# Holding back the taps of a long convolution while stick-breaking weights are worked out, and issuing them more densely around that

## The chip, the cores and the metric

The kernel runs on one core of a Trainium2 chip. The metric is the device time of one execution in microseconds (us). Three executions before the change took 883.54, 887.52 and 886.16 us; their median is 886.16 us. One further execution was profiled.

## What is computed

One layer of an encoder over 512 positions of width 1024. Four branches mix the positions in parallel; what they give is gated, projected, merged and normalised. Two branches matter here: the Conformer convolution, a causal depthwise convolution of 31 taps over 512 channels, and stick-breaking attention with 8 heads of width 64.

```python
g_lin, g_gate = jnp.split(glu, 2, axis=-1)
hB = g_lin * jax.nn.sigmoid(g_gate)
hB = causal_dwconv(hB, conv_dw) + conv_dw_bias      # 31 taps
...
z = jnp.einsum('bhqd,bhsd->bhqs', qi, kh) * scale   # stick-breaking
log_beta = jax.nn.log_sigmoid(z)
log_rest = jnp.where(mask, jax.nn.log_sigmoid(-z), 0.0)
between = lax.cumsum(log_rest, axis=3, reverse=True) - log_rest
att = jnp.where(mask, jnp.exp(log_beta + between), 0.0)
```

## The kernel before, in words

Channels lie on the 128 partitions and the 512 positions along the free axis. Every large projection is done with split operands: a matrix is rounded to a high half (`hi`, on ACT, L108) and the remainder is its low half (`lo`, L109, on DVE, or on POOL for every second piece while `shared[0]` is set), and three products are summed (`mm3`, L121 to L123). A step of a projection is three matmuls of 512 columns. The weights stream in from HBM by SP's queue.

The order of the work is written as generators. `todo` is a list of projections; each `next` of one of them issues a step of three matmuls. `fill(n)` issues n such steps. `chain(gen)` runs a serial computation and calls `fill` with the number that the computation yields, so that TensorE has projection work while it waits for the other engines. Attention is such a computation: `pair` (L730) works on two heads at a time, four pairs in a branch, and yields after each of its three banks of scores (`f1`, 4 steps each and 6 more at the end) and after each of three groups of transposes (`f2_`, 2 steps each and 2 more). Between two pairs `attention` (L799) calls `fill(FB)`, 14 steps.

The convolution's taps ride on `fill`. A tap is one DVE instruction over up to 512 elements (L308 for the first, L310 for the others, `oB` += `hB` shifted times a weight); there are 31 for each of four channel groups, each adding to what the one ahead of it wrote. They wait in the list `taps`, and `fill` pays a fixed share of a tap for every step, in `due`:

```python
if taps:
    due[0] += RATE
    while due[0] >= 1 and taps:
        due[0] -= 1
        taps.pop(0)()
```

With RATE 0.5 one tap goes out for two steps. The taps stand in program order on DVE by `keep_in_program_order`; a scheduler settles the rest of DVE's order.

For a stick-breaking pair the weights of the two heads are worked out in a chain over ACT and DVE. For each bank and head ACT forms two sigmoids from the scores (`rs`, L750, and `a`, L751), DVE runs a reversed cumulative product over `rs` (the scan, L770) and multiplies it into `a` (L771). `rs` has a single buffer, so the next `rs` on ACT waits for the last multiply on DVE. The banks are the 512 long rows, then the 128 and 384 long ones, then the 256 long ones. When the weights stand, TensorE transposes them (L781), ACT copies the transposes, and L796 multiplies them by the values; DVE's L797 takes the result. L665 on DVE multiplies a gated projection into `merged`. L709 and L713 are the low halves of the next pair's queries and keys.

Of the kernel before, what the change touches and what calls it, by code (L numbers as in the profile page):

```python
# [23 lines left out]
F1, F2, FB, FL = (4, 6), (2, 2), 14, (24, 24)  # L24

FE = (10, 2, 8, 34, 2)

RATE = 0.5
O_QA, O_KA, O_VA, O_ZA, O_AA, O_BA = 0, 512, 1024, 1536, 2048, 2052
O_LIN, O_GLU, O_ZB = 2056, 2568, 3080  # L30
O_QC, O_KC, O_VC, O_ZC = 3592, 4104, 4616, 5128
# [45 lines left out]
def trunk(ctx, tc, xT, pT, wi, ws, wb, wo, wg, wp, cst, colp, ln, out):  # L77
# [14 lines left out]
    def nm(p):  # L92
        cnt[0] += 1
        return f"{p}_{cnt[0]}"

    def bank(shape=(128, 512)):
        return psW.tile(list(shape), F32, tag="w", name=nm("w"))
# [45 lines left out]

    taps, due = [], [0.0]

    def fill(n):
        while n > 0 and todo:
            try:
                next(todo[0])
                n -= 1  # L150
                if taps:
                    due[0] += RATE
                    while due[0] >= 1 and taps:
                        due[0] -= 1
                        taps.pop(0)()
            except StopIteration:
                todo.pop(0)

    def finish(gen):

        while gen in todo:
            fill(1)

    def chain(gen):
        for n in gen:
            fill(n)

    def b4(col):
        return col.unsqueeze(2).to_broadcast([128, 4, 128])
# [219 lines left out]
    nc.vector.tensor_tensor(Fst[32:40, :], fc, Fst[0:8, :].bitcast(F32), ALU.subtract)  # L389

    fill(FE[0])
    cum = bank()
    g16f = g16.rearrange("p a b -> p (a b)")
# [103 lines left out]
    def double(cs_):  # L497
# [4 lines left out]
        for i in range(4, 7):  # L502
# [19 lines left out]
            yield 1  # L522

    chain(double((0, 1)))
    chain(double((2, 3)))
    finish(vq[3])

# [172 lines left out]
    def heads(name, pr):  # L700

        pcs = unit(name, pr)
        fox = name == "qkD"
        qs = -0.125 if fox else 0.125
        t = [at.tile([128, T], F32R, tag=n, name=nm(n), bufs=2) for n in ("qh", "ql", "kh", "kl")]

        def qthen(ps):
            nc.scalar.activation(t[0], ps, AF.Copy, scale=qs)
            nc.vector.scalar_tensor_tensor(t[1], ps, qs, t[0].bitcast(F32), ALU.mult, ALU.subtract)  # L709

        def kthen(ps):
            nc.scalar.activation(t[2], ps, AF.Copy)
            nc.vector.tensor_tensor(t[3], ps, t[2].bitcast(F32), ALU.subtract)  # L713

        yield from proj(pcs, 0, qthen)
        yield from proj(pcs, 1, kthen)
        qk[name, pr] = t
        if fox:

            both = base.tile([128, 4, T], F32, tag="oB" if pr % 2 else "hB", name=nm("F"))  # L720
            plain, diag = both[:, 0:2, :], both[:, 2:4, :]
            for hh in range(2):
                ps = acc()
                h = 2 * pr + hh
                mm(ps, lhsT=selr[:, h:h + 1].to_broadcast([128, 128]), rhs=Fst, start=True, stop=True)
                nc.scalar.activation(plain[:, hh, :], ps, AF.Copy)
                nc.gpsimd.tensor_tensor(b3(diag[:, hh, :]), b3(plain[:, hh, :]), h4(far), ALU.add)
            bias[pr] = plain, diag

    def pair(name, pr, v, dst, f1, f2_):  # L730

        fox = name == "qkD"
        qh, ql, kh, kl = qk[name, pr]
        att, aT = {}, {}
        for segs in BANKS:
            pss = [bank(), bank()]
            for i, o in segs:
                n = 128 * (i + 1)
                tq = slice(128 * i, 128 * i + 128)
                for lq, lk in ((qh, kh), (qh, kl), (ql, kh)):  # L740
                    for hh in range(2):
                        ro = slice(64 * hh, 64 * hh + 64)
                        mm(pss[hh][:, o:o + n], lhsT=lq[ro, tq], rhs=lk[ro, 0:n], start=lq is qh and lk is kh, stop=lq is ql)  # L743
            w = max(o + 128 * (i + 1) for i, o in segs)
            for hh in range(2):
                ps = pss[hh]
                a = at.tile([128, T], F32, tag="a", name=nm("a"), bufs=6)
                if not fox:
                    rs = at.tile([128, T], F32, tag="rs", name=nm("rs"), bufs=1)
                    nc.scalar.activation(rs[:, 0:w], ps[:, 0:w], AF.Sigmoid, scale=-1.0)  # L750
                    nc.scalar.activation(a[:, 0:w], ps[:, 0:w], AF.Sigmoid)  # L751
                for i, o in segs:
                    n = 128 * (i + 1)
                    d = o + n - 128
                    if fox:

                        st = at.tile([128, 4], F32, tag="st", name=nm("st"), bufs=6)
                        fp, fd = bias[pr]
                        if i:
                            nc.vector.tensor_tensor_reduce(a[:, o:d], ps[:, o:d], fp[:, hh, 0:n - 128], 1.0, BIG, ALU.add, ALU.min, st[:, 0:1])  # L760
                        nc.vector.tensor_tensor_reduce(a[:, d:o + n], ps[:, d:o + n], fd[:, hh, n - 128:n], 1.0, st[:, 0:1] if i else BIG,
                                                       ALU.add, ALU.min, st[:, 1:2])
                        nc.scalar.activation(a[:, o:o + n], a[:, o:o + n], AF.Exp, bias=st[:, 1:2], scale=-1.0, accum_out=st[:, 2:3])
                        nc.vector.reciprocal(st[:, 3:4], st[:, 2:3])
                        nc.vector.tensor_scalar(a[:, o:o + n], a[:, o:o + n], st[:, 3:4], None, ALU.mult)
                    else:


                        rv = rs[:, o + 1:o + n][:, ::-1]
                        nc.vector.tensor_tensor_scan(rv, rv, last[:, 512 - n:511][:, ::-1], 0.0, ALU.mult, ALU.add)  # L770
                        nc.vector.tensor_tensor(a[:, o:o + n - 1], a[:, o:o + n - 1], rs[:, o + 1:o + n], ALU.mult)  # L771
                        nc.gpsimd.memset(a[:, o + n - 1:o + n], 0.0)
                    att[hh, i] = a[:, o:o + n]
            yield f1[0]
        yield f1[1]
        for n_, segs in enumerate(TBANKS):
            for hh in range(2):
                ps = bank()
                for j, o in segs:
                    for i in range(j, 4):  # L780
                        nc.tensor.transpose(ps[:, o + 128 * (i - j):o + 128 * (i - j) + 128], att[hh, i][:, 128 * j:128 * j + 128], ident)  # L781
                w = max(o + 128 * (4 - j) for j, o in segs)
                t = at.tile([128, T], F32, tag="aT", name=nm("aT"), bufs=6)
                if hh and fox:
                    nc.vector.tensor_copy(t[:, 0:w], ps[:, 0:w])
                else:
                    nc.scalar.activation(t[:, 0:w], ps[:, 0:w], AF.Copy)
                for j, o in segs:
                    aT[hh, j] = t[:, o:o + 128 * (4 - j)]
            yield f2_[0]  # L790
        yield f2_[1]
        po = bank()
        for j in range(4):
            for hh in range(2):
                c0 = 128 * pr + 64 * hh
                mm(po[64 * hh:64 * hh + 64, 128 * j:T], lhsT=v[:, j, c0:c0 + 64], rhs=aT[hh, j], start=j == 0, stop=j == 3)  # L796
        nc.vector.tensor_tensor(dst[:, pr, :], po, dst[:, pr, :], ALU.mult)  # L797

    def attention(name, v, dst, others, first=lambda: None):  # L799
        hs = [heads(name, pr) for pr in range(4)]  # L800
        todo.append(hs[0])
        for pr in range(4):
            finish(hs[pr])
            if pr == 0:
                first()
            if pr < 3:
                todo.append(hs[pr + 1])
            todo.append(others(pr))
            chain(pair(name, pr, v, dst, F1, F2))
            if pr < 3:  # L810
                fill(FB)

    def once(f):
        got = []
# [7 lines left out]
    fill(9999)  # L822

    attention("qkC", v, zC, lambda pr: gates(0, pr, ysA, False, 0))
    while taps:
        taps.pop(0)()
# [43 lines left out]
    todo.append(zbgate())  # L870
    ysB = once(lambda: ysplit(oB, True))
    attention("qkD", v, zD, lambda pr: gates(1, pr, ysB, True, 1), ysB)
    fill(9999)
    s2.close()
# [164 lines left out]
```

## Time and profile before

| | us |
|---|---|
| median of three runs | 886.16 |
| the profiled execution | 883.57 |
| its span, first to last instruction | 881.5 |
| TensorE busy | 850.9 (97%) |
| VectorE (DVE) busy | 552.8 (63%) |
| ScalarE (ACT) busy | 332.7 (38%) |
| GpSimd (POOL) busy | 143.9 (16%) |

A busy share is an average over stages. The four stick-breaking pairs lie between 278 and 416 us of the span. Times in the rows are microseconds from the span's start, and a group's mean is in nanoseconds. L12 is line 12 of the kernel.

### The profile page before, as it was taken

Reading aid. Unit: us, or ns where it says so; the run is one execution under the profiler, and the core shown is the slowest. Engines: PE = TensorE matmul, PEld = TensorE weight load, DVE = VectorE, ACT = ScalarE, POOL = GpSimd, SP = SyncE. Lnnn points to the kernel's source line nnn. Section 1 sums busy time; section 2 is a strip of 40 time slices with the busy share of each in tenths; the row PEclk is TensorE's granted clock in tenths of the full one; section 3 lists DMA queues with packets and bytes.
Section 4 is the critical chain, followed back from the end, with each engine's and each line's share of the span. In section 5 each row is a group of like instructions: output and inputs, shape, how many; then the busy total and the mean of one; then the engine's idle time right before and its main releaser. Section 6 shows DMA issues by size and latency. Waiting matters only on the chain.

```text
span 881.5 us, 11299 instructions
## 1 busy us (share of the span) xinstructions
PE 850.9 (97%) x4364; PEld 685.6 (78%) x4364; DVE 552.8 (63%) x931; ACT 332.7 (38%) x588; POOL 143.9 (16%) x137
## 2 busy tenths in 40 slices
PE   7989999999999999999999999999999999999996
PEld 5767789988897676677898777777788888888885
DVE  4999845569895888886433546374633434454367
ACT  5754322432233444434243434352423323333220
POOL 0453200221122021110122211111111111200021
PEclk9999999999999999999999999999999999999998
DMA  7434411002232121132122312232322222354202
GB/s 253 144 94 128 115 59 49 25 28 93 96 111 96 49 71 52 69 120 72 48 96 96 120 48 72 72 120 72 120 72 92 99 96 74 117 159 152 72 14 83
DMA packets 33653, 79.75 MB, mean 90 GB/s; under 512 B 7104, under 2 KB 13888, under 8 KB 33472
## 3 DMA queue, kind: packets, MB, share of 16 engines
q1 hardware_dynamic: 31152, 73.73, 24.8%
q10 hardware_dynamic: 2448, 5.31, 1.9%
q8 instruction: 34, 0.56, 0.3%
q14 instruction: 19, 0.16, 0.1%
HBM read 74.70 MB, written 4.33 MB: 90 GB/s over the span
## 4 chain that ended last, share of the span: by engine, by line
PE 82%; DVE 10%; issue 2%; ACT 2%; DMA 2%; POOL 2%; SPq 0%; DVEq 0%; ACTq 0%; POOLq 0%
PE p L121 19%; PE p L122 18%; PE p L123 18%; PE w L121 5%; PE w L123 5%; PE w L122 5%; PE w L796 2%; PE w L781 2%; PE w L743 2%; PE w L182 2%; DVE rs L770 1%; PE w L511 1%; PE w L519 1%; DVE lo L109 1%; DVE cacc L272 1%
## 5 line engine op out<-in xcount | busy, mean ns | idle before, releaser
L121 PE MATMUL p<-xhi,hi 128*128 128x512 f32 x656 | 265.8, 405 | 0.0
L122 PE MATMUL p<-xlo,hi 128*128 128x512 f32 x656 | 260.0, 396 | 0.0
L123 PE MATMUL p<-xhi,lo 128*128 128x512 f32 x656 | 259.9, 396 | 0.0
L109 DVE TENSOR_TENSOR lo<-raw,hi 128x1024 fp32r<-128x1024 f32 x114 | 152.2, 1336 | 99.6 <-ACT hi L108 90.3
L108 ACT ACTIVATE hi<-raw 128x1024 fp32r<-128x1024 f32 x124 | 131.0, 1059 | 217.2 <-PE p L122 160.1
L121 PEld LDWEIGHTS p<-xhi,hi 128*128 128x128 f32 x656 | 123.4, 188 | 32.4 <-issue 4.3
L123 PEld LDWEIGHTS p<-xhi,lo 128*128 128x128 f32 x656 | 123.2, 188 | 29.3 <-issue 0.4
L122 PEld LDWEIGHTS p<-xlo,hi 128*128 128x128 f32 x656 | 123.5, 188 | 26.5 <-issue 0.6
L310 DVE SCALAR_TENSOR_TENSOR oB<-hB,cp,oB 128x511 f32<-128x511 f32 (+14 forms) x120 | 97.8, 815 | 2.3
L667 POOL TENSOR_TENSOR merged<-merged,sg 128x512 f32<-128x512 f32 x24 | 34.2, 1427 | 185.1 <-DVE sg L665 113.9
L121 PE MATMUL w<-yh,hi 128*128 128x512 f32 x128 | 51.8, 405 | 0.0
L122 PE MATMUL w<-yl,hi 128*128 128x512 f32 x128 | 50.5, 395 | 0.0
L123 PE MATMUL w<-yh,lo 128*128 128x512 f32 x128 | 50.5, 394 | 0.0
L109 POOL TENSOR_TENSOR lo<-raw,hi 128x1024 fp32r<-128x1024 f32 x10 | 25.5, 2553 | 122.3 <-ACT hi L108 74.8
L665 DVE TENSOR_TENSOR sg<-w,sg 128x512 f32<-128x512 f32 x16 | 11.1, 691 | 41.7 <-PE w L123 41.7
L121 PE MATMUL p<-hi,xhi 128*128 128x256 f32 x128 | 35.8, 280 | 0.0
L770 DVE TENSOR_TENSOR_SCAN rs<-rs,masks 128x511 f32<-128x511 f32 (+3 forms) x32 | 28.6, 913 | 11.5 <-ACT rs L750 11.5
L122 PE MATMUL p<-lo,xhi 128*128 128x256 f32 x128 | 35.7, 279 | 0.0
L123 PE MATMUL p<-hi,xlo 128*128 128x256 f32 x128 | 35.7, 279 | 0.0
L121 PEld LDWEIGHTS w<-yh,hi 128*128 128x128 f32 x128 | 24.0, 188 | 6.3 <-issue 1.0
L123 PEld LDWEIGHTS w<-yh,lo 128*128 128x128 f32 x128 | 24.1, 188 | 5.7
L781 PE MATMUL w<-ident,a 128*128 128x128 f32 x160 | 22.6, 274 | 5.9 <-DVE a L771 5.9
(298 smaller groups left out, 1270.9 us busy)
## 6 DMA issues: line engine op xcount, KB each, us to landing
raw<-wi SPq DMA_DIRECT2D x90, 512.0 KB, 3.2
raw<-wb SPq DMA_DIRECT2D x16, 512.0 KB, 3.2
raw<-wo SPq DMA_DIRECT2D x8, 512.0 KB, 3.1
raw<-wg SPq DMA_DIRECT2D x8, 512.0 KB, 3.3
t<-xT ACTq DMA_DIRECT2D x8, 256.0 KB, 3.3
xr<-xT SPq DMA_DIRECT2D x3, 512.0 KB, 5.5
dX<-Q SPq DMA_DIRECT2D x4, 256.0 KB, 2.6
dL<-L SPq DMA_DIRECT2D x4, 256.0 KB, 2.2
```

The lines of the kernel that those rows point to most:

```text
L108: nc.scalar.activation(hi, raw, AF.Copy)
L109: eng.tensor_tensor(lo, raw, hi.bitcast(F32), ALU.subtract)
L121: mm(ps, lhsT=wh, rhs=ah, start=first, stop=False)
L122: mm(ps, lhsT=wh, rhs=al, start=False, stop=False)
L123: mm(ps, lhsT=wl, rhs=ah, start=False, stop=last)
L182: nc.tensor.transpose(ps[:, 128 * h:128 * h + 128], src(h), idn)
L310: i = nc.vector.scalar_tensor_tensor(a[:, s:], h[:, :T - s], cw31[:, c, 30 - s:31 - s], a[:, s:], ALU.mult, ALU.add)
L667: nc.gpsimd.tensor_tensor(merged[:, d, :], merged[:, d, :], sg, ALU.add)
L743: mm(pss[hh][:, o:o + n], lhsT=lq[ro, tq], rhs=lk[ro, 0:n], start=lq is qh and lk is kh, stop=lq is ql)
L770: nc.vector.tensor_tensor_scan(rv, rv, last[:, 512 - n:511][:, ::-1], 0.0, ALU.mult, ALU.add)
L781: nc.tensor.transpose(ps[:, o + 128 * (i - j):o + 128 * (i - j) + 128], att[hh, i][:, 128 * j:128 * j + 128], ident)
L796: mm(po[64 * hh:64 * hh + 64, 128 * j:T], lhsT=v[:, j, c0:c0 + 64], rhs=aT[hh, j], start=j == 0, stop=j == 3)
```

## The change

`fill` takes the rate as a second argument. While a stick-breaking or forgetting pair works out its weights (the `f1` yields), the rate is HELD, 0: no tap goes out. In the transposes (`f2_`) and in the stretch between pairs (`FB`) it is FREE, 0.9, in place of 0.5. Everywhere else it stays RATE, 0.5. The forgetting branch runs when no taps are left, so that only the stick-breaking branch sees it. The number of taps, of matmuls and of all other instructions is the same.

```diff
--- before.py
+++ after.py
@@ -25,7 +25,7 @@
 
 FE = (10, 2, 8, 34, 2)
 
-RATE = 0.5
+RATE, HELD, FREE = 0.5, 0.0, 0.9
 O_QA, O_KA, O_VA, O_ZA, O_AA, O_BA = 0, 512, 1024, 1536, 2048, 2052
 O_LIN, O_GLU, O_ZB = 2056, 2568, 3080
 O_QC, O_KC, O_VC, O_ZC = 3592, 4104, 4616, 5128
@@ -143,13 +143,13 @@
 
     taps, due = [], [0.0]
 
-    def fill(n):
+    def fill(n, rate=RATE):
         while n > 0 and todo:
             try:
                 next(todo[0])
                 n -= 1
                 if taps:
-                    due[0] += RATE
+                    due[0] += rate
                     while due[0] >= 1 and taps:
                         due[0] -= 1
                         taps.pop(0)()
@@ -163,7 +163,7 @@
 
     def chain(gen):
         for n in gen:
-            fill(n)
+            fill(*n) if isinstance(n, tuple) else fill(n)
 
     def b4(col):
         return col.unsqueeze(2).to_broadcast([128, 4, 128])
@@ -771,8 +771,8 @@
                         nc.vector.tensor_tensor(a[:, o:o + n - 1], a[:, o:o + n - 1], rs[:, o + 1:o + n], ALU.mult)
                         nc.gpsimd.memset(a[:, o + n - 1:o + n], 0.0)
                     att[hh, i] = a[:, o:o + n]
-            yield f1[0]
-        yield f1[1]
+            yield f1[0], HELD
+        yield f1[1], HELD
         for n_, segs in enumerate(TBANKS):
             for hh in range(2):
                 ps = bank()
@@ -787,8 +787,8 @@
                     nc.scalar.activation(t[:, 0:w], ps[:, 0:w], AF.Copy)
                 for j, o in segs:
                     aT[hh, j] = t[:, o:o + 128 * (4 - j)]
-            yield f2_[0]
-        yield f2_[1]
+            yield f2_[0], FREE
+        yield f2_[1], FREE
         po = bank()
         for j in range(4):
             for hh in range(2):
@@ -808,7 +808,7 @@
             todo.append(others(pr))
             chain(pair(name, pr, v, dst, F1, F2))
             if pr < 3:
-                fill(FB)
+                fill(FB, FREE)
 
     def once(f):
         got = []
```

The matmuls, the POOL and the DMA instructions stand in the same order as before. On ACT one rounding (L108) stands behind a pair of sigmoids where it stood ahead of them. The rest of the difference is on DVE.

The first place is on DVE, the end of the first pair's weights: the two 256 long rows. Before, taps (L310) stand among them:

```order
L310 SCALAR_TENSOR_TENSOR oB<-hB,cp,oB 128x508
L770 SCALAR_TENSOR_TENSOR rs_2561<-rs_2561,masks 128x255
L310 SCALAR_TENSOR_TENSOR oB<-hB,cp,oB 128x507
L771 TENSOR_TENSOR a_2560<-a_2560,rs_2561 128x255
L709 SCALAR_TENSOR_TENSOR ql_2486<-p_2489,qh_2485 128x512
L310 SCALAR_TENSOR_TENSOR oB<-hB,cp,oB 128x506
L770 SCALAR_TENSOR_TENSOR rs_2568<-rs_2568,masks 128x255
L310 SCALAR_TENSOR_TENSOR oB<-hB,cp,oB 128x505
L771 TENSOR_TENSOR a_2567<-a_2567,rs_2568 128x255
```

Now:

```order
L709 SCALAR_TENSOR_TENSOR ql_2486<-p_2489,qh_2485 128x512
L770 SCALAR_TENSOR_TENSOR rs_2557<-rs_2557,masks 128x255
L771 TENSOR_TENSOR a_2556<-a_2556,rs_2557 128x255
L770 SCALAR_TENSOR_TENSOR rs_2564<-rs_2564,masks 128x255
L771 TENSOR_TENSOR a_2563<-a_2563,rs_2564 128x255
```

The four taps are gone from the chain, and `ql` (L709) stands ahead of both scans rather than between them.

The second place is on DVE, the stretch between the third pair and the fourth, from the first L665 behind the third pair's L797 to the fourth pair's first multiply. Before, where one more tap (128x488) stands between that L797 and the first row:

```order
L665 TENSOR_TENSOR merged<-w_3336,sg_3267 128x512
L310 SCALAR_TENSOR_TENSOR oB<-hB,cp,oB 128x487
L310 SCALAR_TENSOR_TENSOR oB<-hB,cp,oB 128x486
L310 SCALAR_TENSOR_TENSOR oB<-hB,cp,oB 128x485
L310 SCALAR_TENSOR_TENSOR oB<-hB,cp,oB 128x484
L310 SCALAR_TENSOR_TENSOR oB<-hB,cp,oB 128x483
L310 SCALAR_TENSOR_TENSOR oB<-hB,cp,oB 128x482
L109 TENSOR_TENSOR lo_3446<-raw_3443,hi_3445 128x1024
L665 TENSOR_TENSOR merged<-w_3393,sg_3362 128x512
L109 TENSOR_TENSOR lo_3640<-raw_3637,hi_3639 128x1024
L770 SCALAR_TENSOR_TENSOR rs_3417<-rs_3417,masks 128x511
L771 TENSOR_TENSOR a_3416<-a_3416,rs_3417 128x511
```

Now the stretch begins, right behind L797, with

```order
L310 SCALAR_TENSOR_TENSOR oB<-hB,cp,oB 128x495
L665 TENSOR_TENSOR merged<-w_3328,sg_3258 128x512
L310 SCALAR_TENSOR_TENSOR oB<-hB,cp,oB 128x494
L310 SCALAR_TENSOR_TENSOR oB<-hB,cp,oB 128x493
L310 SCALAR_TENSOR_TENSOR oB<-hB,cp,oB 128x492
L310 SCALAR_TENSOR_TENSOR oB<-hB,cp,oB 128x491
L310 SCALAR_TENSOR_TENSOR oB<-hB,cp,oB 128x490
L310 SCALAR_TENSOR_TENSOR oB<-hB,cp,oB 128x489
L310 SCALAR_TENSOR_TENSOR oB<-hB,cp,oB 128x488
L310 SCALAR_TENSOR_TENSOR oB<-hB,cp,oB 128x487
```

and goes on with

```order
L109 TENSOR_TENSOR lo_3445<-raw_3442,hi_3444 128x1024
L310 SCALAR_TENSOR_TENSOR oB<-hB,cp,oB 128x486
L665 TENSOR_TENSOR merged<-w_3390,sg_3356 128x512
L310 SCALAR_TENSOR_TENSOR oB<-hB,cp,oB 128x485
L109 TENSOR_TENSOR lo_3640<-raw_3637,hi_3639 128x1024
L310 SCALAR_TENSOR_TENSOR oB<-hB,cp,oB 128x484
L770 SCALAR_TENSOR_TENSOR rs_3416<-rs_3416,masks 128x511
L310 SCALAR_TENSOR_TENSOR oB<-hB,cp,oB 128x483
L771 TENSOR_TENSOR a_3415<-a_3415,rs_3416 128x511
```

Twelve taps stand where seven stood, and one more between the scan and the multiply. In the two stretches before it, behind the first and the second pair's L797, the taps ahead of the next scan go from nine to twelve each; in the second of them one of the twelve is a group's first tap (L308), and one more tap stands between the scan and the multiply. In the second pair three taps leave the chain and in the third three; the fourth had none.

## Rows read from the trace of the kernel before

**Rows 1.** The page, busy times and granted clock over the span.
```profile
PE 850.9 (97%) x4364; PEld 685.6 (78%) x4364; DVE 552.8 (63%) x931; ACT 332.7 (38%) x588; POOL 143.9 (16%) x137
...
PEclk9999999999999999999999999999999999999998
```
**Rows 2.** Waits of PE, longest first: us in total, times, longest.
```profile
PE w L781 <- DVE a L771: 5.9, 5, 2.2
```
**Rows 3.** PE in order of time, transposes of pairs 1 to 4: start, length, [idle before].
```profile
295.86 0.55 PE L781 MATMUL w<-ident,a 128*128 128x128 f32 x3 [2.17 <-DVE a L771]
...
331.70 0.66 PE L781 MATMUL w<-ident,a 128*128 128x128 f32 x4 [0.32 <-DVE a L771]
333.85 0.55 PE L781 MATMUL w<-ident,a 128*128 128x128 f32 x3 [1.49 <-DVE a L771]
...
369.75 0.66 PE L781 MATMUL w<-ident,a 128*128 128x128 f32 x4 [0.41 <-DVE a L771]
371.92 0.55 PE L781 MATMUL w<-ident,a 128*128 128x128 f32 x3 [1.51 <-DVE a L771]
...
407.13 1.04 PE L781 MATMUL w<-ident,a 128*128 128x128 f32 x8
...
413.59 2.37 PE L796 MATMUL w<-aT,v 128*64 128x512 f32 x16
```
**Rows 4.** DVE in order of time, the first pair's weights.
```profile
282.02 0.69 DVE L771 TENSOR_TENSOR a<-a,rs 128x511 f32<-128x511 f32 x1
...
294.76 0.72 DVE L310 SCALAR_TENSOR_TENSOR oB<-hB,cp,oB 128x505 f32<-128x505 f32 x1
295.39 0.41 DVE L771 TENSOR_TENSOR a<-a,rs 128x255 f32<-128x255 f32 x1
```
**Rows 5.** DVE in order of time, the stretch behind pair 1 and pair 2's weights.
```profile
307.91 8.23 DVE L310 SCALAR_TENSOR_TENSOR oB<-hB,cp,oB 128x496 f32<-128x496 f32 x8
...
317.79 2.82 DVE L770 TENSOR_TENSOR_SCAN rs<-rs,masks 128x511 f32<-128x511 f32 x1
320.72 0.69 DVE L771 TENSOR_TENSOR a<-a,rs 128x511 f32<-128x511 f32 x1
322.13 1.22 DVE L770 TENSOR_TENSOR_SCAN rs<-rs,masks 128x511 f32<-128x511 f32 x1 [0.73 <-ACT rs L750]
...
333.38 0.42 DVE L771 TENSOR_TENSOR a<-a,rs 128x255 f32<-128x255 f32 x1
```
**Rows 6.** DVE in order of time, pair 3's first and last multiply.
```profile
358.75 0.69 DVE L771 TENSOR_TENSOR a<-a,rs 128x511 f32<-128x511 f32 x1
...
371.44 0.42 DVE L771 TENSOR_TENSOR a<-a,rs 128x255 f32<-128x255 f32 x1
```
**Rows 7.** DVE in order of time, pair 4's weights: no tap among them.
```profile
394.99 0.69 DVE L771 TENSOR_TENSOR a<-a,rs 128x511 f32<-128x511 f32 x1
...
404.27 0.69 DVE L770 TENSOR_TENSOR_SCAN rs<-rs,masks 128x255 f32<-128x255 f32 x1 [0.53 <-ACT rs L750]
...
406.79 0.42 DVE L771 TENSOR_TENSOR a<-a,rs 128x255 f32<-128x255 f32 x1
```
**Rows 8.** POOL in order of time: the splits of low halves ahead of pair 2.
```profile
310.92 2.40 POOL L109 TENSOR_TENSOR lo<-raw,hi 128x1024 fp32r<-128x1024 f32 x1 [17.09 <-ACT hi L108]
316.57 2.97 POOL L109 TENSOR_TENSOR lo<-raw,hi 128x1024 fp32r<-128x1024 f32 x1 [3.25 <-ACT hi L108]
```
**Rows 9.** PE in order of time, the first matmuls of the span.
```profile
4.86 0.80 PE L121 MATMUL w<-xhi,wh 128*128 128x512 f32 x1 [4.86 <-ACT wh L232]
...
8.02 0.62 PE L121 MATMUL w<-xhi,wh 128*128 128x512 f32 x1
8.45 0.43 PE L122 MATMUL w<-xlo,wh 128*128 128x512 f32 x1
8.72 0.39 PE L123 MATMUL w<-xhi,wl 128*128 128x512 f32 x1
8.95 0.40 PE L121 MATMUL w<-xhi,wh 128*128 128x512 f32 x1
```

## Prediction, made before the changed kernel had run

> **What bounds the kernel now.** I read the page first: PE is busy for 850.9 of 881.5 us, DVE for 552.8, and the granted clock is at 0.9 or more of full speed in all slices but the last [rows 1]. So PE's queue is the path, its order does not change, and the time can change only by what PE waits. The list of waits comes next: the one between PE and the stick-breaking weights is the largest there, 5.9 us in five waits, for L771 [rows 2]. PE's timeline places them: 2.17 us in pair 1, 0.32 and 1.49 in pair 2, 0.41 and 1.51 in pair 3, none in pair 4 [rows 3]. They add up to the 5.9. That is the most that a shorter chain could give. The last thing to read is DVE's timeline around each pair [rows 4 to 7], since every one of these waits ends when the last multiply of a pair ends.
>
> What the reader is to see there: in pair 4 no tap is in the way, and from the start of the first multiply to the end of the last the chain takes 407.21 - 394.99 = 12.2 us, with short waits for ACT in it, 0.53 ahead of a 256 long scan [rows 7]. In pair 1 the same stretch takes 295.80 - 282.02 = 13.8 [rows 4], in pair 2 333.80 - 320.72 = 13.1 [rows 5], in pair 3 371.86 - 358.75 = 13.1 [rows 6]. So three or four taps cost the chain 0.9 or 1.6 us only; the rest of them runs where DVE waits for ACT anyway. And the first scan of pair 2 follows a row of taps [rows 5]: the queue ahead of the chain is full.
>
> **The change part by part.** A tap costs 0.63 us on DVE when another instruction follows (294.76 to 295.39 [rows 4]). In a row of taps each waits for the one ahead of it; eight take 8.23 us, of which some 2.1 are a block by POOL (below), so 0.76 each [rows 5].
>
> *Taps out of the chain.* Pair 1: its first multiply does not move, so its last one ends at 282.02 + 12.2 + 0.1 = 294.3 in place of 295.8. The 0.1 is `ql`, 0.6 long, now in a wait of 0.53. PE gains 1.5 of its 2.17 us. Pairs 2 and 3: 13.1 to 12.3, a gain of 0.8 each. Pair 4: nothing.
>
> *Taps into the queue ahead of the chain.* Behind L797 PE's progress sets DVE's start, so this stretch moves with PE, and then every added tap stands ahead of the scan. The order counts them: before pair 2 twelve for nine, 3 x 0.76 = 2.3 us. Before pair 3 twelve for nine, one of them short, 2.1, and one between scan and multiply, 0.6: 2.7. Before pair 4 twelve for seven, two in a row and three alone, 2 x 0.76 + 3 x 0.63 = 3.4, and one between scan and multiply, 0.6: 4.0.
>
> *The sum.* Pair 1 leaves PE 1.5 ahead. Pair 2: -1.5 + 2.3 - 0.8 = 0.0: its last multiply ends when it ended before, and the lead is waited away. Pair 3: 0.0 + 2.7 - 0.8 = +1.9. Pair 4: its second four transposes had nothing to wait for; the eight begin at 407.13 [rows 3], the last multiply ends at 407.21 [rows 7], and half of the eight come first, so some 0.4 is spare: 1.9 + 4.0 - 0.4 = +5.5. Behind pair 4 PE has no wait for DVE in this branch, so nothing gives it back. **+5.5 us**: 883.57 + 5.5 = 889.1 for the profiled execution. The median shown is 886.16, 2.6 above that execution; +5.5 on it is 891.7, which I give.
>
> *Costed at nothing.* The halves that DVE splits off (L109) stand behind more taps. What covers them is the projection that runs before their unit is due: the list of waits has no wait of PE for L109, and the extra taps are 2 to 4 us. If that cover were gone, PE would wait for L109, by up to those 2 to 4 us a pair. The rounding on ACT that goes behind two sigmoids of 256 is moved by about the length of these and feeds the same later unit. L665 and L797 free banks of PSUM somewhat later; with PE itself later, I see no new wait in it, only the same delay under another name. The same 124 taps run, and no DMA moves in its queue.
>
> *The unknown: POOL's splits.* In the stretch behind a pair POOL forms a low half, 2.40 us from 310.92, inside the row of eight taps, and another from 316.57, which is 2.97 long [rows 8]; the scan that starts at 317.79 takes 2.82 where its twin takes 1.22 [rows 5]. So each split blocks DVE: the second costs 2.82 - 1.22 = 1.6 us, the first 8.23 - 8 x 0.76 = 2.1. I take both as before, on a tap or on the scan, since both stand ahead of the first multiply. Between the ends: if the second split meets DVE while it waits, 1.6 is saved in each of pairs 2 and 3; if it takes a whole 2.1 in place of 1.6, 0.5 is lost in each. The tap's price has its ends at 0.63 and 0.76: seven in rows at the lower one would take off 0.9, six alone at the upper one add 0.8. The two taps between scan and multiply cost nothing if they fit into a wait, 1.2 less. Without any spare in pair 4, 0.4 more. I take for each tap the row that has it in the same company.
>
> This is where a rule would change the sign. In these rows POOL gets in between two taps and DVE is the one that waits. The Trainium skill, SBUF — State Buffer, section Who interferes with whom, says that a DVE instruction with two SBUF inputs and a GpSimd instruction that reads SBUF lock each other out, and that "Issue order, not op shape, decides who blocks." By the row the sum is +5.5; by the rule with DVE always first it is the second rival.
>
> **The rivals.**
>
> *A block leaves the queue.* PE and the splits shift against DVE's taps, and POOL's second split in the stretches ahead of pairs 2 and 3 falls where DVE waits. For it: DVE has such waits, 0.73 between multiply and scan [rows 5]. Against it: more taps leave fewer of them. 5.5 - 2 x 1.6 = +2.3: 888.5.
>
> *The taps win against POOL.* A denser row of taps holds POOL off, and POOL's 2.1 and 1.6 us ahead of pairs 2 and 3 and its 2.1 ahead of pair 4 no longer stand in DVE's queue. That outweighs the extra taps (2.3, 2.7 and 4.0) in the first two and half of them in the third, and the waits fall towards what is left in pair 1, 0.67 a pair: 3 x 0.67 = 2.0 of 5.9, so -3.9: 882.3, not slower. It decides from the point where the first scan of a pair waits for ACT and not for DVE's queue. For it speaks that the 2.97 is longer than the 2.40, so POOL has waited for DVE too; against it that it got in after one instruction both times [rows 5, 8].
>
> *The change does more than it says.* All of the 5.9 us goes, 880.3. The order speaks against it: the taps taken out of the chains come back right ahead of them.
>
> *The clock falls.* After its first wait of 4.86 us PE runs a matmul of 512 columns in 0.43 us from start to start, later in 0.23 [rows 9], which are the two levels of 1.2 and 2.4 GHz. The waits up to 2.17 us in rows 3 left it at the upper level. Pair 4 now gets waits that it did not have; if the clock fell there, the work from 407.13 to the end of L796 at 415.96 [rows 3] would take up to 8.8 us longer: 900.5. By my working no single wait is much over 3 us. Its chance rests on rows 9 alone, where PE ran at the lower level behind a wait. The Trainium skill, TensorE: Matmul & The Clock Gate, section What's actually happening, says that an idle array goes back to half rate; no row here shows a fall behind work, so by the rows the clock adds nothing and by the rule up to the 8.8.
>
> **How the numbers follow.** A measurement of this kernel tells about 0.5% from no change, 4.4 us. The forecast gets 0.63. With the ends above it lies between 5.5 - 0.9 - 1.2 = +3.4 and 5.5 + 1.0 + 0.8 + 0.4 = +7.7, and 0.07 of its chance under 4.4 us. The block that leaves the queue gets 0.27, all of it within 0.5%. The taps that win get 0.05; that time, too, is within 0.5% by a little, and I split it in 0.02 faster and 0.03 not. All of the 5.9 gone gets 0.02, faster; the clock 0.03, slower. Slower 0.59, within 0.5% 0.37, faster 0.04. The range runs from the lower rival less the spread of a median of three (886.16 - 883.54 = 2.6), 888.5 - 2.6 = 885.9, to the upper end of the forecast and as much as the runs shown lie above their median (1.36), 886.16 + 7.7 + 1.4 = 895.3. It leaves out the taps that win, all of it gone, and the clock.
>
> **What would show it.** In the profile after, pair 1's wait for L771 is about 0.7 us, and the last multiply of a pair follows the first by 12.2 or 12.3 us in all four pairs. Ahead of pair 4's first scan DVE shows no wait, and its last multiply ends near 413 us. PE's waits for L771, with any for `a` on ACT's side in the same pairs, add up to about 11.4. If DVE stands waiting for ACT ahead of the first scans of pairs 2 to 4, the queue was not full and the sum is wrong. If PE waits for L109 or L713, what I costed at nothing is wrong. If all of that holds and the time is the same, time outside of these pairs has moved.

## The result: 0.8% slower, and the profile after

The changed kernel takes 893.15 us (median of six executions, 891.42 to 894.75); the kernel before, on the same chip, 886.43 (883.54 to 887.52). The ratio is 1.0079, with an interval of 1.0058 to 1.0099. The predicted 891.7 us is 1.5 below what was measured, and the range held it.

The profiled execution took 892.35 us, its span is 890.3: 8.8 more than the 881.5 of before. The page's busy times and granted clock, as in [rows 1]:

```profile
PE 855.2 (96%) x4364; PEld 689.0 (77%) x4364; DVE 552.5 (62%) x931; ACT 332.8 (37%) x588; POOL 143.7 (16%) x137
...
PEclk9999999999999999899999999999999999999998
```

TensorE does the same 4364 matmuls and is busy for 4.3 us longer, and in the seventeenth slice the granted clock is an 8. So there are two things to find: what PE (TensorE) waits, and where its clock fell. The list of waits answers the first, as in [rows 2]:

```profile
PE w L781 <- DVE a L771: 10.8, 7, 2.6
...
PE w L121 <- ACT a L751: 0.4, 1, 0.4
```

Together 11.2 us where 5.9 stood: 5.3 more. DVE in order of time shows where they come from. Before, the rows of L797 behind pairs 1, 2 and 3 were these:

```profile
305.66 0.69 DVE L797 TENSOR_TENSOR zC<-w,zC 128x512 f32<-128x512 f32 x1 [2.05 <-PE w L796]
...
343.62 0.69 DVE L797 TENSOR_TENSOR zC<-w,zC 128x512 f32<-128x512 f32 x1 [1.61 <-PE w L796]
...
381.71 0.69 DVE L797 TENSOR_TENSOR zC<-w,zC 128x512 f32<-128x512 f32 x1 [1.34 <-PE w L796]
```

Now: the first pair's first and last multiply, the stretch behind it with the second pair's weights, L797 and the first and last multiply around pair 3, and the stretch ahead of the fourth pair with its weights (it answers to [rows 4, 5, 6, 7]):

```profile
280.97 0.69 DVE L771 TENSOR_TENSOR a<-a,rs 128x511 f32<-128x511 f32 x1
...
292.76 0.42 DVE L771 TENSOR_TENSOR a<-a,rs 128x255 f32<-128x255 f32 x1
...
303.03 0.69 DVE L797 TENSOR_TENSOR zC<-w,zC 128x512 f32<-128x512 f32 x1 [1.66 <-PE w L796]
...
305.29 8.27 DVE L310 SCALAR_TENSOR_TENSOR oB<-hB,cp,oB 128x502 f32<-128x502 f32 x8
...
314.61 2.88 DVE L310 SCALAR_TENSOR_TENSOR oB<-hB,cp,oB 128x494 f32<-128x494 f32 x1
317.41 0.68 DVE L665 TENSOR_TENSOR merged<-w,sg 128x512 f32<-128x512 f32 x1
318.01 1.48 DVE L310 SCALAR_TENSOR_TENSOR oB<-hB,cp,oB 128x493 f32<-128x493 f32 x2
319.42 1.22 DVE L770 TENSOR_TENSOR_SCAN rs<-rs,masks 128x511 f32<-128x511 f32 x1
320.73 0.69 DVE L771 TENSOR_TENSOR a<-a,rs 128x511 f32<-128x511 f32 x1
...
332.53 0.42 DVE L771 TENSOR_TENSOR a<-a,rs 128x255 f32<-128x255 f32 x1
...
344.14 0.69 DVE L797 TENSOR_TENSOR zC<-w,zC 128x512 f32<-128x512 f32 x1 [3.26 <-PE w L796]
...
361.93 0.69 DVE L771 TENSOR_TENSOR a<-a,rs 128x511 f32<-128x511 f32 x1
...
373.71 0.42 DVE L771 TENSOR_TENSOR a<-a,rs 128x255 f32<-128x255 f32 x1
...
386.83 0.69 DVE L797 TENSOR_TENSOR zC<-w,zC 128x512 f32<-128x512 f32 x1 [4.69 <-PE w L796]
...
402.01 1.22 DVE L770 TENSOR_TENSOR_SCAN rs<-rs,masks 128x511 f32<-128x511 f32 x1
403.15 0.70 DVE L310 SCALAR_TENSOR_TENSOR oB<-hB,cp,oB 128x483 f32<-128x483 f32 x1
403.76 0.69 DVE L771 TENSOR_TENSOR a<-a,rs 128x511 f32<-128x511 f32 x1
...
415.36 0.66 DVE L665 TENSOR_TENSOR merged<-w,sg 128x512 f32<-128x512 f32 x1
415.94 0.41 DVE L771 TENSOR_TENSOR a<-a,rs 128x255 f32<-128x255 f32 x1
```

Read it in two halves. From the first multiply of a pair to the end of its last the chain is now 12.2 us in pairs 1 to 3, shorter, as the change means it; in pair 4, which had no tap to lose, it is 12.6 where it was 12.2. From L797 to the first multiply it is 17.7, 17.8 and 16.9 us ahead of pairs 2, 3 and 4, and the scans at 319.42 and 402.01 show no idle time ahead of them: DVE's queue is full there. Before, these stretches were 15.1, 15.1 and 13.3.

POOL's second split ahead of pair 2 is this row, as in [rows 8]:

```profile
313.90 3.05 POOL L109 TENSOR_TENSOR lo<-raw,hi 128x1024 fp32r<-128x1024 f32 x1 [3.19 <-ACT hi L108]
```

It now falls on a tap (2.88 us at 314.61) and not on the scan, which is back at 1.22 from 2.82 [rows 5]. The block changed its victim and stayed in the queue, and it grew: from the tap's start to the next instruction's are 2.80 us where a tap alone takes 0.63, so it costs 2.2 us, where it cost the scan 1.6.

PE in order of time at the transposes, as in [rows 3], shows the waits and what follows them:

```profile
293.24 0.55 PE L781 MATMUL w<-ident,a 128*128 128x128 f32 x3 [0.78 <-DVE a L771]
...
331.28 0.66 PE L781 MATMUL w<-ident,a 128*128 128x128 f32 x4 [2.53 <-DVE a L771]
333.01 0.90 PE L781 MATMUL w<-ident,a 128*128 128x128 f32 x3 [1.07 <-DVE a L771]
333.56 0.78 PE L121 MATMUL p<-xhi,hi 128*128 128x512 f32 x1
334.14 0.63 PE L122 MATMUL p<-xlo,hi 128*128 128x512 f32 x1
334.56 0.63 PE L123 MATMUL p<-xhi,lo 128*128 128x512 f32 x1
...
372.47 0.66 PE L781 MATMUL w<-ident,a 128*128 128x128 f32 x4 [2.60 <-DVE a L771]
374.19 0.90 PE L781 MATMUL w<-ident,a 128*128 128x128 f32 x3 [1.07 <-DVE a L771]
...
414.30 0.66 PE L781 MATMUL w<-ident,a 128*128 128x128 f32 x4 [1.27 <-DVE a L771]
416.41 0.55 PE L781 MATMUL w<-ident,a 128*128 128x128 f32 x3 [1.45 <-DVE a L771]
```

In pairs 2 and 3 there are two waits, 2.53 or 2.60 and then 1.07, with four short transposes between them. Behind the second one three transposes take 0.90 in place of 0.55, and matmuls of 512 columns follow each other by 0.42 us (334.14 to 334.56), where the first matmuls of the span show 0.43 [rows 9]. That is the lower level of the clock. A view by stretches has the granted clock (the columns: the stretch and its length, busy time and count of PE, weight load, DVE, ACT and POOL, the granted clock, the DMA share, GB/s):

```profile
329.00:333.00 4.00, 0.66 (x4) 0.42 (x4) 3.28 (x8) 2.34 (x6) 0.20 (x2) 0.94 0.01 4
333.00:337.00 4.00, 3.99 (x18) 3.42 (x18) 3.93 (x6) 2.57 (x5) 0.00 (x0) 0.63 0.40 127
370.00:374.00 4.00, 0.66 (x4) 0.42 (x4) 3.28 (x8) 2.15 (x6) 0.20 (x2) 0.94 0.00 0
374.00:378.00 4.00, 3.81 (x12) 3.13 (x13) 3.93 (x6) 2.51 (x5) 0.00 (x0) 0.50 0.37 130
378.00:382.00 4.00, 4.00 (x20) 3.50 (x19) 3.93 (x6) 1.69 (x4) 0.00 (x0) 0.71 0.22 66
```

What the clock took is the missing share of the stretches in which PE works: 0.37 x 4 = 1.5 us behind pair 2 and (0.50 + 0.29) x 4 = 3.2 behind pair 3, less 0.1 for the 0.19 in which PE still waits there: 4.5 together. The 0.06 in the stretches ahead of these cost nothing: there the clock fell in about the last half microsecond of the wait of 1.07, while PE stood idle. So the 8.8 us of the span are 5.3 of waits and 4.5 of clock, less 1.05 ahead of pair 1, whose first multiply starts at 280.97 where it started at 282.02 in the execution of before [rows 4].

### The profile page after: what moved, and what is told of

Its sections match the earlier page's. It is cut to its first block, busy times and chain, and to the rows that moved or that the text cites. A ratio compares the mean times of both kernels' runs of the same rounds, so it can differ in the third digit from the quotient of the medians.

```text
span 890.3 us, 11297 instructions
## 1 busy us (share of the span) xinstructions
PE 855.2 (96%) x4364; PEld 689.0 (77%) x4364; DVE 552.5 (62%) x931; ACT 332.8 (37%) x588; POOL 143.7 (16%) x137
## 4 chain that ended last, share of the span: by engine, by line
PE 79%; DVE 13%; issue 2%; ACT 2%; DMA 2%; POOL 2%; SPq 0%; DVEq 0%; ACTq 0%; POOLq 0%
PE p L121 18%; PE p L122 18%; PE p L123 18%; PE w L121 4%; PE w L123 4%; PE w L122 4%; DVE oB L310 2%; PE w L796 2%; PE w L781 2%; PE w L182 2%; DVE rs L770 2%; PE w L743 2%; DVE a L771 2%; PE w L511 1%; PE w L519 1%
## 5 line engine op out<-in xcount | busy, mean ns | idle before, releaser
L109 DVE TENSOR_TENSOR lo<-raw,hi 128x1024 fp32r<-128x1024 f32 x114 | 152.0, 1334 | 99.2 <-ACT hi L108 90.2
L108 ACT ACTIVATE hi<-raw 128x1024 fp32r<-128x1024 f32 x124 | 130.8, 1059 | 216.7 <-PE p L122 161.1
L310 DVE SCALAR_TENSOR_TENSOR oB<-hB,cp,oB 128x511 f32<-128x511 f32 (+14 forms) x120 | 102.2, 851 | 2.5
L109 POOL TENSOR_TENSOR lo<-raw,hi 128x1024 fp32r<-128x1024 f32 x10 | 25.5, 2554 | 124.1 <-ACT hi L108 74.2
L665 DVE TENSOR_TENSOR sg<-w,sg 128x512 f32<-128x512 f32 x16 | 11.1, 692 | 40.9 <-PE w L123 40.9
L781 PE MATMUL w<-ident,a 128*128 128x128 f32 x160 | 24.5, 288 | 10.8 <-DVE a L771 10.8
L770 DVE TENSOR_TENSOR_SCAN rs<-rs,masks 128x511 f32<-128x511 f32 (+3 forms) x32 | 25.4, 816 | 13.0 <-ACT rs L750 13.0
L781 PEld LDWEIGHTS w<-ident,a 128*128 128x128 f32 x160 | 19.9, 148 | 16.0 <-DVE a L771 12.8
```

What stands on the lines that cost most here:

```text
L108: nc.scalar.activation(hi, raw, AF.Copy)
L109: eng.tensor_tensor(lo, raw, hi.bitcast(F32), ALU.subtract)
L310: i = nc.vector.scalar_tensor_tensor(a[:, s:], h[:, :T - s], cw31[:, c, 30 - s:31 - s], a[:, s:], ALU.mult, ALU.add)
```

## The experiments

Nine kernels ran, each beside the kernel before on the same chip (its median was 885.65 to 885.99 us there). The theory from the prediction: time is what stands in DVE's queue between L797 and a pair's first scan, and the taps put there are the loss. The rivals: holding the taps back is what costs, the clock is the loss and not the waits, or the number of taps hardly matters beside POOL's splits. In the table "waits" are PE's for the weights (on L771, and on ACT's `a` where there is such a wait) in the profiled execution, "taps" those from an L797 to the next pair's first multiply. The granted clock is the mean over an execution, once for the profiled one and once as the median of all executions of the kernel (for the kernel before, the 48 beside the experiments; 885.65 is the median of the first 14). Each ratio is to the kernel before in its own group. A thousandth of the clock is some 0.9 us of an execution: an estimate, 0.001 of 886, and the figures have no finer step.

| kernel | median us | ratio to before (interval) | waits us | clock, profiled | clock, median |
|---|---|---|---|---|---|
| before: 9, 9 and 7 taps | 885.65 | 1 | 5.9 | 0.997 | 0.993 |
| after: 12, 13 and 13 taps | 893.15 | 1.0079 (1.0058 to 1.0099) | 11.2 | 0.992 | 0.991 |
| held, no denser rate | 878.97 | 0.9925 (0.9913 to 0.9937) | 1.9 | 0.998 | 0.9965 |
| denser, not held | 895.53 | 1.0108 (1.0088 to 1.0127) | 12.4 | 0.988 | 0.988 |
| after, waits of pairs 2 and 3 filled | 888.25 | 1.0040 (1.0025 to 1.0056) | 4.9 | 0.993 | 0.997 |
| before, no splits on POOL | 881.01 | 0.9948 (0.9934 to 0.9962) | 3.4 | 0.994 | 0.994 |
| held, denser in the transposes alone | 878.84 | 0.9932 (0.9919 to 0.9946) | 1.9 | 0.998 | 0.9975 |
| held, denser between pairs alone | 893.57 | 1.0096 (1.0081 to 1.0110) | 10.5 | 0.992 | 0.990 |
| held, denser rate 0.7 | 884.87 | 0.9990 (0.9980 to 1.0001) | 5.4 | 0.994 | 0.996 |
| held, no splits on POOL | 880.77 | 0.9945 (0.9932 to 0.9959) | 2.3 | 0.995 | 0.994 |
| after, no splits on POOL | 885.78 | 0.9999 (0.9989 to 1.0009) | 6.3 | 0.992 | 0.9935 |

**One half of the change alone: hold the taps back, and issue them at the old rate everywhere else.**

```diff
-RATE, HELD, FREE = 0.5, 0.0, 0.9
+RATE, HELD, FREE = 0.5, 0.0, 0.5
```

> The change with FREE at 0.5 in place of 0.9: taps are still held while the weights are worked out, but go out no more densely than before around that. In the order 7 taps stand ahead of the next scan behind each L797 (9, 9 and 7 before, 12 in the changed kernel), none in the chains, and 17 are left over for the end of the branch. Queue theory (the denser rate filled DVE's queue ahead of the chain, and that alone made the changed kernel slower): PE's waits for L771 fall from 5.9 us to about 1 us, the granted clock stays at 1.00 around the four pairs, and the time is 4.5 to 5.5 us below the kernel before, near 881, ratio 0.994 to 0.995. Rival (holding taps is itself the loss, since they are missing later): the 17 left over delay the convolution's layer norm, PE waits there, and the time is that of before or above, 886 to 893.

Measured: 878.97 us, 0.9925 of before and 6.7 us under it, more than the 4.5 to 5.5 expected. The list of waits, and DVE ahead of pair 2:

```profile
PE w L781 <- DVE a L771: 1.9, 3, 0.8
```
```profile
304.48 0.69 DVE L797 TENSOR_TENSOR zC<-w,zC 128x512 f32<-128x512 f32 x1 [4.00 <-PE w L796]
...
315.95 2.87 DVE L770 TENSOR_TENSOR_SCAN rs<-rs,masks 128x511 f32<-128x511 f32 x1 [0.75 <-ACT rs L750]
318.93 0.69 DVE L771 TENSOR_TENSOR a<-a,rs 128x511 f32<-128x511 f32 x1
```

With seven taps in this stretch DVE stands idle for 0.75 us ahead of the scan: the queue is no longer full. POOL's block is back on the scan. Holding back is a gain of its own, 4.0 us of wait (5.9 to 1.9) in the profiled execution; the rest goes with the clock, 0.9965 in the median against 0.9925 of before beside it, some 3.5 us by estimate. The taps left over run behind pair 4, where PE does not wait for DVE.

**The other half alone: the denser rate, without holding back.**

```diff
-RATE, HELD, FREE = 0.5, 0.0, 0.9
+RATE, HELD, FREE = 0.5, 0.5, 0.9
```

> The change with HELD at 0.5 in place of 0: nothing is held, only the denser rate of 0.9 in the transposes and between the pairs is left. Queue theory: twelve taps stand ahead of the scans of pairs 2 and 3 and three or four in the chains as before, so PE's waits for L771 grow to about 13 us (5.9 before, 10.8 in the changed kernel), each of the longer ones over 3 us, the granted clock falls in pairs 2 and 3, and the time is 7 to 13 us above the kernel before, 893 to 899. Pair 4 has no taps left and waits for nothing. Rival (holding is the loss): without it the time is that of the kernel before, 886 to 888.

Measured: 895.53 us, ratio 1.0108: the loss is the denser rate's, and holding back takes some of it off. The profile has five waits of 12.4 us together and the lowest mean clock, 0.988. In pair 1 it has a wait that can be laid beside one of before:

```profile
294.29 0.63 PE L781 MATMUL w<-ident,a 128*128 128x128 f32 x3 [2.17 <-DVE a L771]
294.59 0.76 PE L121 MATMUL p<-xhi,hi 128*128 128x512 f32 x1
```

The stretch from 294 to 298 us, with the columns as above, shows the clock:

```profile
294.00:298.00 4.00, 3.71 (x13) 3.05 (x14) 4.00 (x7) 0.62 (x2) 0.00 (x0) 0.58 0.23 56
```

The same 2.17 us before the same transposes as in [rows 3], where these three took 0.55 and the clock of this stretch was 1.00; here they take 0.63, and the clock falls.

**Denser in the transposes alone, and denser between the pairs alone.** The first leaves `fill(FB)` at 0.5, the second gives 0.9 to it alone:

```diff
-                fill(FB, FREE)
+                fill(FB)
```
```diff
-RATE, HELD, FREE = 0.5, 0.0, 0.9
+RATE, HELD, FREE = 0.5, 0.0, 0.5
...
-                fill(FB, FREE)
+                fill(FB, 0.9)
```

> The change with the denser rate of 0.9 in the transposes alone; between the pairs the rate is 0.5. The order has 7 taps behind each L797 ahead of the next scan (12 in the changed kernel, 7 in the run that only holds), 7 ahead of L797 (7 and 4), none in the chains, and 9 left at the end of the branch (1 and 17). Queue theory, sharpened (only taps behind L797 count, since ahead of it DVE waits for PE anyway): same time as the run that only holds, 878 to 880, ratio 0.991 to 0.994, waits for L771 about 2 us, no fall of the clock in the four pairs. Rival (a denser rate costs wherever it stands, by DVE's load or by POOL's port): between that run and the changed kernel, 883 to 889.

> The change with the denser rate of 0.9 between the pairs alone; in the transposes it is 0.5. Twelve taps stand behind each L797 ahead of the next scan as in the changed kernel, 4 ahead of L797 in place of 7, 5 are left at the end. Queue theory, sharpened: waits for L771 of 10 to 11 us, the clock falls behind those of pairs 2 and 3, and the time is the changed kernel's or up to 2 us less, 891 to 894, ratio 1.006 to 1.010. Rival (the taps ahead of L797 count too): the time is clearly under the changed kernel's, 884 to 889.

Measured: 878.84 us and 893.57. The first is the same as holding back alone, the second the same as the change. Taps ahead of L797 cost nothing, since there DVE waits for PE in any case (4.00 us in the row of L797 of the first experiment); the whole loss is in the taps behind it.

**How many taps the stretch holds.**

```diff
-RATE, HELD, FREE = 0.5, 0.0, 0.9
+RATE, HELD, FREE = 0.5, 0.0, 0.7
```

> The change with FREE at 0.7 in place of 0.9. Ten taps stand behind each L797 ahead of the next scan (9, 9 and 7 before; 7 with 0.5, 12 with 0.9), none in the chains. By taps alone, at 0.76 us each and three pairs, the waits lie between those of 0.5 (1.9 us) and of 0.9 (11.2): about 6.5, so that the time without any fall of the clock is near that of before, 885 to 887. If the loss of clock comes only with waits as long as the changed kernel's (2.5 and 1.1 us behind each other), the time is 884 to 887, ratio 0.998 to 1.002, and most of the way from 0.5 to 0.9 lies above it; if the clock falls behind these waits too, 888 to 891, ratio 1.003 to 1.006.

Measured: 884.87 us. Seven taps a stretch gave 879.0, ten 884.9, twelve or thirteen 893.15. By the queue alone three taps of 0.63 to 0.76 us in three stretches are 5.7 to 6.8, and the step from seven to ten is 5.9, with the clock at 0.9965 and 0.996 in the median. A step of two or three more gave 8.3, and there the clock has its part: 0.991, some 4.4 us by estimate. In the profiled execution of this kernel the clock did fall once, in pair 2, in the work that followed waits of 1.11 and 1.07 us (granted clock 0.66 from 334 to 338 us).

**POOL's splits.** The kernel before with every low half formed on DVE:

```diff
-    shared[0] = True
+    shared[0] = False
```

> The kernel before, with the low halves of this branch all on DVE and none on POOL: in each stretch behind a pair two splits of 1.14 us stand in DVE's queue in place of POOL's two. Block theory (POOL's two splits hold up a tap for 2.1 us and a scan for 1.6): 3.7 us go, 2.3 come, PE's waits for L771 in pairs 2 and 3 fall from 1.8 and 1.9 to about 0.6 each, and the time is 2 to 3 us below the kernel before, 883 to 884.5, ratio 0.9965 to 0.998. Rival (the long tap and scan have another cause, or POOL's work was free): DVE has 2.3 us more ahead of each chain, the waits grow by up to that in pairs 2 and 3, and the time is 3 to 5 us above.

Measured: 881.01 us, ratio 0.9948, more than expected. DVE ahead of pair 2:

```profile
309.68 3.04 DVE L310 SCALAR_TENSOR_TENSOR oB<-hB,cp,oB 128x496 f32<-128x496 f32 x4
312.65 1.23 DVE L109 TENSOR_TENSOR lo<-raw,hi 128x1024 fp32r<-128x1024 f32 x1
...
319.47 1.22 DVE L770 TENSOR_TENSOR_SCAN rs<-rs,masks 128x511 f32<-128x511 f32 x1
```

Four taps take 3.04, 0.76 each, and the scan 1.22: no block is left. Each split costs DVE some 1.2 us itself and 1.6 to 2.2 when POOL does it beside taps, so DVE is better off doing it. Waits went from 5.9 to 3.4 us, which is 2.5 of the 4.6 that the medians are apart. The clock, 0.994 in the median against 0.9925 of before beside it, makes some 1.3 more by estimate; the remaining 0.8 stay open.

The same edit on the changed kernel and on the one that only holds back:

> The changed kernel with all low halves formed on DVE, so that POOL's blocks of 2.1 and 1.65 us leave the denser rows of taps and a DVE instruction of 1.22 us comes in the place of each. Theory, blocks and taps stand in one queue and add: some 1.3 us less of wait in each of pairs 2 and 3 and about as much in pair 4, waits for L771 from 10.8 to about 7 us, and, if the shorter waits leave the clock up in pairs 2 and 3, up to 5 us more: 884 to 889.5 us. Rival, the number of taps alone makes the loss, whatever stands between them: 892 to 894 us.

Measured: 885.78 us, 7.4 below the changed kernel, within what the theory gave and not the rival's 892 to 894. Waits of 6.3 us are 4.9 less, and the clock, 0.9935 in the median against 0.991, is some 2.2 by estimate. It is no clean price for the blocks, though: the order moved too. Ten and eleven taps stand ahead of the scans of pairs 2 to 4 in place of twelve, and in pair 2 a tap and a split stand behind the first multiply, inside the chain. That the queue gets shorter with the blocks alone is shown on the kernel before, where the nine, nine and seven taps stayed: from L797 to the first multiply are 13.4 us ahead of pairs 2 and 3, where 15.1 stood. In the profiled execution (0.992) the clock fell in pair 1, behind a wait of 2.15, and far ahead of the pairs (0.79 from 108 to 116 us), but not in pairs 2 and 3.

> The first experiment's kernel (taps held back during the weights, no denser rate elsewhere) with all low halves formed on DVE. Theory, the chain's queue is what counts: with the taps held back and not put elsewhere the waits for L771 were down to 1.9 us, so taking POOL's blocks away as well can give at most those 1.9 us more: 877.0 to 879.0 us, waits for L771 between 0 and 1.9 us. Rival, the two gains are of different places and add: 6.7 us from holding back and 4.6 us from POOL's splits, some 874.4 us. Rival, the low halves on DVE now hold up something else that holding back had not touched: above 879.6 us, with a wait of PE for L109.

Measured: 880.77 us, slower than with POOL's splits (878.97), above what either the first theory or the first rival gave. It is the last rival's time, but not its mechanism: PE has no wait for L109 in the list. DVE and then PE in order of time, the end of pair 1's weights:

```profile
293.06 1.23 DVE L109 TENSOR_TENSOR lo<-raw,hi 128x1024 fp32r<-128x1024 f32 x1
294.20 0.68 DVE L770 TENSOR_TENSOR_SCAN rs<-rs,masks 128x255 f32<-128x255 f32 x1
294.80 0.73 DVE L310 SCALAR_TENSOR_TENSOR oB<-hB,cp,oB 128x510 f32<-128x510 f32 x1
295.44 0.42 DVE L771 TENSOR_TENSOR a<-a,rs 128x255 f32<-128x255 f32 x1
```
```profile
295.92 0.88 PE L781 MATMUL w<-ident,a 128*128 128x128 f32 x3 [2.15 <-DVE a L771]
```

A split on DVE and a tap ended up inside the chain, ahead of the last scan and the last multiply. It is the fault that holding back had mended, made again by another instruction: the wait is 2.15 us, and the clock fell behind it (the three transposes take 0.88). Over all executions the clock is 0.994 in the median against 0.9965 with POOL's splits, some 2.2 us by estimate, and the times are 1.8 apart.

**The clock by itself.** The changed kernel with matmuls of 512 columns ahead of the transposes of the first bank in pairs 2 and 3, nine for the first head and four for the second. What they write is overwritten by the transposes; nothing is left out.

```diff
             for hh in range(2):
                 ps = bank()
+                if not fox and n_ == 0 and pr in (1, 2):
+                    for _ in range(9 if hh == 0 else 4):
+                        mm(ps, lhsT=xhi[:, 0, 0:128], rhs=xhi[:, 0, :], start=True, stop=True)
```

> The changed kernel with 9 and 4 matmuls of 512 columns, whose result is overwritten, ahead of the first transposes of the first and second head in pairs 2 and 3 only. They take 9 x 0.233 = 2.1 and 4 x 0.233 = 0.9 us and fit in the waits of 2.53, 1.07, 2.60 and 1.07 us that stand there, so PE is busy where it waited and DVE's queue is the same. Clock theory (part of the loss is the clock that fell to half for 3.41 and 6.83 us behind these waits): the granted clock stays at 1.00 there, and the time comes down by 3.5 to 5 us from the changed kernel's, to 888 to 890, ratio to before 1.002 to 1.004. Rival (the fall costs nothing, since DVE's chain sets the end of the next pair): same time as the changed kernel, 892 to 894, or a little more for the added work, ratio 1.007 to 1.010.

Measured: 888.25 us, 4.9 below the changed kernel, although it does more work on PE. PE in pair 2:

```profile
329.47 2.23 PE L781 MATMUL w<-xhi 128*128 128x512 f32 x9
...
332.29 0.55 PE L784 MATMUL w<-ident,a 128*128 128x128 f32 x3 [0.47 <-DVE a L771]
```

The transposes wait for the same multiply, with PE busy in most of the wait, and three of them take 0.55 again. So in these two places the clock costs the changed kernel some 4.9 us, near the 4.5 from the stretches, and the clock of all executions says the same: 0.997 in the median against 0.991. It is not the clock's share of the 6.7 us between the changed kernel and the kernel before, whose own clock is 0.993. In this kernel's profiled execution (890.44 us, above its median) the clock fell elsewhere, in pair 4's second wait among others:

```profile
412.00:416.00 4.00, 2.76 (x8) 2.35 (x9) 2.95 (x5) 1.86 (x3) 0.00 (x0) 0.57 0.04 8
```

The waits there are 1.28 and 1.46. In the changed kernel's execution the clock did not fall behind its own (1.27 and 1.45).

## Why the prediction was right, and which term was wrong

**What bounds the kernel** held: the waits for L771 are where the time went and where the clock fell, and PE has no wait for L109 or L713 after the change either.

**Taps out of the chain** held. Pair 1's last multiply comes 1.6 us earlier against its own first (1.5 forecast), its wait is 0.78 (0.7), and pairs 2 and 3 give back 0.9 each (0.8). Denser taps ahead of L797 cost nothing, as the sum had it without saying so.

**Taps into the queue** held nearly to the tenth. From L797 to the first multiply the rows of before and after differ by 2.6, 2.7 and 3.7 us; 2.3, 2.7 and 4.0 were forecast, 9.0 together in both. The tenths are in part luck: in pair 2 the three added taps took 2.0 us and not 2.3 (1.41 for the two from 318.01 to the scan, and 0.63), and POOL's second block took 0.5 more than its 1.6, the end that I had named and not taken; pair 3 shows the same (two taps and a block take 3.67 us from 355.32). The 0.76 for a tap in a row and the 2.1 for a block I had worked out from each other; the four taps in 3.04 us of the kernel without POOL's splits show the 0.76 by themselves. In pair 4 the chain itself grew by 0.4, by the L665 at 415.36 that stands in front of its last multiply. The waits came to 11.2 us against 11.4.

**POOL's splits** were taken as before, on a tap or on the scan, and the rows show them so, the second one dearer. "A block leaves the queue" did not happen. "The taps win against POOL" did not either: in the denser rows POOL got in again (8.27 us for eight taps, 8.23 before). The Trainium skill, SBUF — State Buffer, section Who interferes with whom, says that issue order decides who blocks; the rows agree, since the split that starts at 313.90 stands ahead of the tap of 314.61, and DVE is the one that waits.

**The clock** is the term that failed. I costed it at nothing, gave its fall a chance of 0.03, and looked for it in pair 4 alone. It fell in the second of the two waits of pair 2 and of pair 3 and took 4.5 us, and since slow matmuls also bring L797 later, by 1.4 and 2.9 us (10.2 or 10.3 from a pair's last multiply to L797 before; 11.6 and 13.1 now), everything behind moved with it. That is why pair 4's last multiply ends at 416.4 and not near 413: counted from pair 1's first multiply it is 10.2 us late, 6.0 by taps and blocks, where I had 5.9, and 4.2 by the clock. The step of the argument that was wrong was to judge by the longest single wait ("no single wait is much over 3 us", and 2.17 had left the clock up). I had also read every wait of a pair as ending with its last multiply, but the first of two ends with the multiply before that, so that a longer queue makes two waits close to each other: in pairs 2 and 3 PE waits 2.5 and 1.1 us with 0.7 us of short work between. And 2.17 itself was followed by a fall in another kernel. The Trainium skill, TensorE: Matmul & The Clock Gate, section What's actually happening, says that an idle array goes back to the lower level, and that the hardware's look at it is "free-running"; the rows now agree with the first, and the second would account for the same wait ending differently from one execution to another. No run here shows that by itself.

**The time** came out 1.5 above the forecast and not 5 because the two comparisons differ: the medians are 6.7 apart, the profiled executions 8.8. The profiled execution of before (883.57) lies 2.9 under its kernel's median, with a clock of 0.997 that had not fallen ahead of the last slice. Other executions of before do lose time to the clock: of the 48 beside the experiments the four at 0.996 or 0.997 took 882.2 to 883.9 us, the seven at 0.991 took 886.2 to 888.0, and the median is 0.993. So between the medians, 0.993 and 0.991, the clock makes some 1.8 us by estimate and not 4.5. The range held the time in part by luck: the +5.5 was put on a median that had such a loss in it already.

## What to carry to other kernels

Work that is off the path should go where its engine waits for the bound engine anyway (here ahead of L797), and not behind the instruction that restarts a serial chain: there every instruction ahead of the chain's first link counts in full once the queue has no idle time left. So count, stretch by stretch, what the queue can hold: here seven taps left it idle time, and the next three cost 5.9 us. Then price a new wait on TensorE at more than its length, because the clock may fall with it, and look at the granted clock of every execution before one profiled execution is laid beside another.

The version to keep is the half of the change that holds the taps back, at the old rate elsewhere: 878.97 us, ratio 0.9925 to before and 14.2 us under the change.

## What the runs showed of the hardware that was not expected

The clock fell in the second of two waits of 2.53 and 1.07 us with four short transposes between them. Behind a wait of 2.17 us it fell in one kernel and stayed up in another, and behind two near 1.4 us it stayed up in the changed kernel and fell, at the same place, in the kernel with filled waits. The plainest case is one that the change does not touch: near 108 us PE waits 1.8 to 2.0 us for a load in all eleven profiled executions (L182), and the clock fell behind it in three of them, with waits of 1.78, 1.91 and 2.01, and stayed up in eight, with 1.81 to 2.03. So the length of such a wait does not tell whether the clock falls. A profiled execution tells what a fall costs, and only the granted clock of several executions tells how often it comes.

Forming a low half on POOL was dearer for DVE than doing it on DVE: the split takes DVE 1.2 us, and POOL's holds a tap or a scan up by 1.6 to 2.2 us. Moving all of them to DVE gained 4.6 us in the kernel before.
